# A two-layer convolution and delta-net mixer: the output's gate is spread over the partitions through DRAM instead of by products on TensorE

## The chip, the cores and the metric

The kernel runs on one core of one Trainium2 chip, which has engines for products (TensorE, "PE"; its weight loads are "PEld"), for elementwise work (VectorE, "DVE", and ScalarE, "ACT"), for general work (GpSimd, "POOL") and for issuing transfers (SyncE, "SP"). The metric is the time of one launch on the device in microseconds, lower is better. There is one core, so it is also the slowest.

## The reference, cut to what matters

Two layers (DEPTH = 2) work on 1024 tokens `x` and 256 context tokens `ctx` of 1024 channels. Each layer modulates a normalized input, projects it, runs a convolution branch and a gated delta rule of four heads, and adds the gated output projection:

```python
def modulate(x, cond, norm_w, w_ada, b_ada):
    mod = jax.nn.silu(cond) @ w_ada + b_ada
    shift, scale, gate = (jnp.expand_dims(m, -2) for m in jnp.split(mod, 3, axis=-1))
    return rms_norm(x, norm_w) * (1 + scale) + shift, gate
...
    h, gate = modulate(x, cond, norm_w, w_ada, b_ada)
    proj = h @ w_in
...
    out = jnp.concatenate([y_conv, y_dn], axis=-1) @ w_out
    return x + gate * out, s_f, s_b
```

So `gate` is one vector of 1024 numbers for each layer and condition (`c` for `x`, `c_ctx` for `ctx`). It multiplies every token's output row, channel by channel. The context has no output in the last layer, so layer 1 needs the gate for `x` alone.

## The kernel before, in words

The 1280 tokens stand in 10 blocks of 128. For each layer, 28 groups of projection weights (128 columns each) are streamed through three buffers `wst` by transfers on SP's queue, split by ScalarE (`whi`) and VectorE (`wlo`) into a 16-bit high and low part, and multiplied by the input's high and low part in three products for each of 8 slices (L376; 128x512 or 128x256).

A layer consists of steps. For head h these are K, Q, V and Z (projections; Z also writes the output gate `sgz` to `gdr` in DRAM), A (`head_a`, convolutions and norms of Q, K, V, with what the decay needs), B (`head_b1`: a 32x32 elimination on VectorE, L701 to L713, with the transposes L712 and L713 at its end, then the block inverse by small products from L729 on), D (`head_b2`, transposes and masks), R (`head_rec`, the recurrence over 10 blocks in both directions, L845 to L881) and N (`head_norm`, L894 to L924). For the convolution branch they are C (projection of a slice), T (the taps on VectorE, L528 and L538), L (`conv_norm`, layer norm of a block of tokens) and G (the convolution's gate: `sgc` to `gdr`). W (`early_wout`) loads the first two slices of the output weights. The string PLAN[l] lists the steps in the order in which they are written, and LEAD gives some of them a lead over others: the framework then sets one fixed program for each engine, in which instructions with a lead stand earlier. An engine runs its program in order, so an instruction that waits holds up all behind it.

The modulation is computed in 24 groups of 128 columns. A group's weights are loaded by `ada_load` and used by `ada_use` (L164: products with the condition; L181: VectorE adds the bias and writes two columns of `md`, one for each condition). Groups 16 to 23 are the gate. ADA_AT[l] lists the weight groups of the projection after which a modulation group is taken.

At the end of a layer comes the output: for each block of 128 tokens, `y` is loaded from `ydr` on SP (L1003), ScalarE and VectorE split it into `yh` and `yl` (L1010, L1011), the output weights are split into `woh` and `wol` (L414, L415), TensorE takes three products for each of 8 slices and two halves of 512 columns (L1022, into `pj` or `rc`), and `out_end` multiplies them by the gate (L1034, `tmp = pj * gbc`) and adds `x` (L1035). The last head's part of `y` never goes to DRAM: `head_norm` leaves it in `olast`, with eight products (L918) to spread the norm. The first two blocks are done together, and their products for the first three slices come first.

`gbc[v]` is a tile of 128x1024 with the gate of condition v on every partition (L1066 to L1075). Since `md` has the channels on the partitions, the tile is made on TensorE: for each half of 512 columns, four products take one column of `md`, repeated 128 times, as the weights and the identity as the moving side (L1071), and ScalarE copies the PSUM bank into the tile (L1074):

```python
pe.matmul(pg[:, k * 128:(k + 1) * 128],
          lhsT=md[l][:, 16 + hf * 4 + k, v:v + 1].to_broadcast([128, 128]), rhs=ident,
          start=True, stop=True)
```

Layer 0 does it for both conditions, layer 1 for one: 24 products and 6 copies. The trace keeps two records for a product of this type (4-byte operands, 128 columns).

Of the kernel before, what the change touches and what calls it, by code (L numbers as in the profile page):

```python
# [8 lines left out]
F32 = mybir.dt.float32  # L9
# [4 lines left out]
AF = mybir.ActivationFunctionType  # L14
# [4 lines left out]
DEPTH = 2  # L19
# [23 lines left out]
for _name, _w in (("nw", DEPTH * KT), ("bada", DEPTH * 24), ("cw", DEPTH * 4 * CW), ("cb", DEPTH * 4),  # L43
# [7 lines left out]


PLAN = (
# [4 lines left out]
)  # L58

ADA_AT = ((0, 2, 4, 6, 7, 8, 9, 10, 11, 12, 13, 14, 15, 16, 17, 18, 19, 20, 21, 22, 23, 24, 26, 27), (0, 3, 10, 14, 15, 16, 19, 22))


LEAD = {'O': 300, 'A': 700, 'B': 450, 'D': 1000, 'L': 1200, 'M': 0, 'N': 500, 'R': 1000, 'W': 2550}


def pos(b):
# [4 lines left out]
def mixer_kernel(ctx: ExitStack, tc: tile.TileContext, xs, cst_d, wada, win, wab, gp_d, wout, fnw, out):  # L73
    nc = tc.nc
    dve, act, pool, pe = nc.vector, nc.scalar, nc.gpsimd, nc.tensor
# [6 lines left out]
    def bank(tag, bufs, shape=(128, 512)):  # L82
        return ps.tile(list(shape), F32, tag=tag, name=tag, bufs=bufs)

    def misc(shape=(128, 512)):
        return bank("pb", 2, shape)
# [14 lines left out]
    ident = cp.tile([128, 128], F32, name="ident")  # L101
# [21 lines left out]
    xres = tc.dram_tile([T, DM], F32, name="xres")  # L123
    ydr = [tc.dram_tile([KT - 1, 128, T], F32, name=f"ydr{l}") for l in range(DEPTH)]
    cdr = [tc.dram_tile([4, 128, T], F32, name=f"cdr{l}") for l in range(DEPTH)]
    gdr = [tc.dram_tile([KT, 128, T], F32, name=f"gdr{l}") for l in range(DEPTH)]
    rdr = [tc.dram_tile([20, T], F32, name=f"rdr{l}") for l in range(DEPTH)]

# [28 lines left out]
    def bada(l, g0, g1):  # L157
        b0 = _COLS["bada"] + 24 * l
        return cst[:, b0 + g0:b0 + g1].unsqueeze(2).to_broadcast([128, g1 - g0, 2])

    def ada_mm(o, w):

        for k in range(KT):
            pe.matmul(o, lhsT=w[:, k, :], rhs=scond[:, k:k + 1, :].to_broadcast([128, 64, 2]), start=(k == 0),  # L164
                      stop=(k == KT - 1))
# [5 lines left out]
    md = [gp.tile([128, 24, 2], F32, tag=f"md{l}", name=f"md{l}") for l in range(DEPTH)]  # L171

    def ada_load(l, g):
        w = wp.tile([128, KT, 128], F32, tag="wst", name="wst", bufs=3)
        nc.sync.dma_start(w, wada[l, g])
        return l, g, w

    def ada_use(l, g, w):
        pa = bank("pw", 1, (128, 64, 2))
        ada_mm(pa, w)  # L180
        dve.tensor_tensor(out=md[l][:, g:g + 1, :], in0=pa[:, 0:1, :], in1=bada(l, g, g + 1), op=ADD)  # L181

    def ada_mod(l):
        n0 = _COLS["nw"] + KT * l
        m = md[l]
        nwb = cst[:, n0:n0 + KT].unsqueeze(2).to_broadcast([128, KT, 2])
        dve.scalar_tensor_tensor(out=m[:, 8:16, :], in0=m[:, 8:16, :], scalar=1.0, in1=nwb, op0=ADD, op1=MUL)
        dve.tensor_scalar(out=m[:, 8:16, :], in0=m[:, 8:16, :], scalar1=32.0, scalar2=None, op0=MUL)
        ss = gp.tile([128, 2], F32, tag="mss", name="mss")
        jk = gp.tile([128, 16], F32, tag="mjk", name="mjk")  # L190
        for v in range(2):
            act.activation(jk, m[:, 0:16, v], AF.Square, accum_out=ss[:, v:v + 1])
        pq = bank("pw", 1, (128, 2))
        pe.matmul(pq, lhsT=ones, rhs=ss, start=True, stop=True)
        s, inv = pow2(pq, 2, "mh")
        inv4 = gp.tile([128, 4], F32, tag="inv4", name="inv4", bufs=2)
        for i_ in range(2):
            dve.tensor_scalar(out=inv4[:, 2 * i_:2 * i_ + 2], in0=inv, scalar1=(1.0, 0.5)[i_], scalar2=None, op0=MUL)
        ab = gp.tile([128, 16, 2], F32, tag="ab", name="ab", bufs=2)
        dve.tensor_tensor(out=ab, in0=m[:, 0:16, :], in1=s.unsqueeze(1).to_broadcast([128, 16, 2]), op=MUL)  # L200
        return ab, inv4
# [129 lines left out]
    def later(n, f, *a):  # L331
        for _ in range(n):
            yield 1
        f(*a)
# [9 lines left out]
    def load_w(l, g, invh):  # L344
        prefetch((l, g))
        split((l, g))
        nxt_ = GORDER.index((l, g)) + 1

        if held:
            active.append(later(0, ada_use, *held.pop()))  # L350
        if nxt_ < len(GORDER) and GORDER[nxt_][0] == l:
            prefetch(GORDER[nxt_])
            active.append(later(0, split, GORDER[nxt_]))
        if (nxt_ - 1) % (len(GORDER) // DEPTH) in ADA_AT[l]:
            held.append(ada_load(*ADA[l].pop(0)))
        hi, lo, inv, _ = ready.pop((l, g))
        return hi, lo, unscale(inv, invh)
# [40 lines left out]
    for l in range(DEPTH):  # L398
# [65 lines left out]
        g = gp.tile([128, NB, 8], F32, tag="gg", name="gg")  # L464
# [464 lines left out]
        def emit(step):  # L929
            k, i = step[0], int(step[1:] or 0)  # L930
            if k in "KQV":
                head_proj(i, "KQV".index(k))
            elif k == "A":
                with after("elim"):
                    prep[i] = head_a(i)
            elif k == "B":
                inv[i] = head_b1(i, prep[i][0], prep[i][2])
            elif k == "D":
                b2[i] = head_b2(i, *prep[i])
            elif k == "R":  # L940
                head_rec(i, prep[i][0], prep[i][2], inv[i], *b2[i])
            elif k == "N":
                head_norm(i, prep[i][0], b2[i][2][:, 1], b2[i][3], zs[i])
            elif k == "Z":
                zs[i] = head_z(i)
            elif k == "C":
                us[i] = conv_proj(i)
            elif k == "T":
                with after("elim"):
                    conv_taps(i // 3, i % 3)  # L950
            elif k == "G":
                conv_gate(i)
            elif k == "W":
                early_wout()
            elif k == "L":
                conv_norm(i)

        for step in PLAN[l].split():
            with tc.high_priority(LEAD[step[0]]) if step[0] in LEAD else nullcontext():
                emit(step)  # L960
        while active:
            tick()
        while held:
            ada_use(*held.pop())
# [6 lines left out]
        with tc.tile_pool(name=f"op{l}", bufs=1, side="right", reuse_waits="tile") as op:  # L971
            spare = {}

            def place(tag, n=DM, dt=F32):
                if tag in spare:
                    return spare.pop(tag)[:, 0:n]
                t_ = op.tile([128, n], dt, tag=tag, name=tag, bufs=1)
                return t_[:, 0:n]
# [13 lines left out]
            def out_tile(tt, tag):  # L992
                i = (tt - xb0) % 2
                y = place(f"y{i}", 896).rearrange("p (k t) -> p k t", t=128)
                yh, yl = (place(f"{t_}{i}", DM, F32R).rearrange("p (k t) -> p k t", t=128) for t_ in ("yh", "yl"))
                return tt, y, yh, yl, [bank(tag, 2) for _ in range(2)]
# [57 lines left out]
            gbc = {}  # L1054

            with tc.high_priority(LEAD["O"]):
                two = [out_tile(xb0, "pj"), out_tile(xb0 + 1, "rc")]
# [6 lines left out]
                for k in KORDER[NEARLY + 3:]:  # L1064
                    load_wout(place, k)
            for v in ((0,) if last else (1, 0)):  # L1066
                t_ = place(f"gb{v}")
                for hf in range(2):
                    pg = misc()
                    for k in range(4):  # L1070
                        pe.matmul(pg[:, k * 128:(k + 1) * 128],  # L1071
                                  lhsT=md[l][:, 16 + hf * 4 + k, v:v + 1].to_broadcast([128, 128]), rhs=ident,
                                  start=True, stop=True)
                    act.activation(t_[:, hf * 512:(hf + 1) * 512], pg, AF.Copy)  # L1074
                gbc[v] = t_  # L1075
            if last:
                fw = place("fw")
                nc.sync.dma_start(fw, fnw.partition_broadcast(128))
# [87 lines left out]
```

## Time and profile before

| | |
|---|---|
| median of three runs | 1574.67 us (1572.23 to 1576.7) |
| profiled execution, its own time | 1572.46 us |
| its span | 1570.8 us |
| TensorE busy | 1457.3 us, 93% |
| VectorE busy | 1253.7 us, 80% |
| ScalarE busy | 896.0 us, 57% |
| POOL busy | 145.1 us, 9% |
| granted clock of TensorE, mean | 0.976 |

A share of busy time is a mean over stages with different limits. A timeline row has the start, the length, the engine, the line and operation, the tiles with their shape and a count of equal rows in succession, and in brackets how long the engine stood idle ahead of it and for whom. A clock of 1.00 means 2.4 GHz and 0.50 means 1.2 GHz.

### The profile page before, as it was taken

Reading aid. Unit: us, or ns where it says so; the run is one execution under the profiler, and the core shown is the slowest. Engines: PE = TensorE matmul, PEld = TensorE weight load, DVE = VectorE, ACT = ScalarE, POOL = GpSimd, SP = SyncE. Lnnn points to the kernel's source line nnn. Section 1 sums busy time; section 2 is a strip of 40 time slices with the busy share of each in tenths; the row PEclk is TensorE's granted clock in tenths of the full one; section 3 lists DMA queues with packets and bytes.
Section 4 is the critical chain, followed back from the end, with each engine's and each line's share of the span. In section 5 each row is a group of like instructions: output and inputs, shape, how many; then the busy total and the mean of one; then the engine's idle time right before and its main releaser. Section 6 shows DMA issues by size and latency. Waiting matters only on the chain. (4 is left out here: it accounts for less than half of the span.)

```text
span 1570.8 us, 27515 instructions
## 1 busy us (share of the span) xinstructions
PE 1457.3 (93%) x10536; PEld 991.6 (63%) x10536; DVE 1253.7 (80%) x2759; ACT 896.0 (57%) x2013; POOL 145.1 (9%) x252
## 2 busy tenths in 40 slices
PE   7899899899998999899899999999899799999997
PEld 1656577577655776676787754476467476467686
DVE  3865989899679999856676556999999989987675
ACT  3757467565347764645454337576676577576321
POOL 0002010100011101101000002010110100121000
PEclk9799999999999999999999999999999999999999
DMA  9213111311143213333743113121311312253651
GB/s 299 113 55 109 45 62 54 138 45 55 58 135 108 76 54 106 112 135 124 250 156 104 55 41 110 39 75 44 112 62 41 121 54 69 82 175 120 213 171 54
DMA packets 83328, 158.21 MB, mean 101 GB/s; under 512 B 5670, under 2 KB 52764, under 8 KB 83196
## 3 DMA queue, kind: packets, MB, share of 16 engines
q1 hardware_dynamic: 67408, 96.74, 19.8%
q0 software_dynamic: 15280, 59.52, 10.3%
q8 instruction: 83, 1.36, 0.3%
q14 instruction: 49, 0.40, 0.1%
q10 hardware_dynamic: 508, 0.19, 0.0%
HBM read 125.43 MB, written 30.99 MB: 100 GB/s over the span
## 5 line engine op out<-in xcount | busy, mean ns | idle before, releaser
L376 PE MATMUL pj<-hhi,whi 128*128 128x512 f16 (+1 forms) x1184 | 424.8, 359 | 4.2 <-ACT raw L596 3.9
L376 PE MATMUL pj<-hhi,wlo 128*128 128x512 f16 (+1 forms) x1184 | 424.4, 359 | 1.2 <-DVE wlo L300 1.1
L376 PE MATMUL pj<-hlo,whi 128*128 128x512 f16 (+1 forms) x1184 | 425.2, 359 | 0.0
L376 PEld LDWEIGHTS <-whi 128*128 128x128 f16 x2368 | 231.5, 99 | 179.3 <-issue 20.2
L538 DVE SCALAR_TENSOR_TENSOR acc<-u,cws,acc 128x960 f32<-128x960 f32 (+26 forms) x240 | 231.0, 963 | 1.2
L376 PEld LDWEIGHTS <-wlo 128*128 128x128 f16 x1184 | 117.4, 99 | 90.5 <-issue 7.9
L1022 PE MATMUL pj<-woh,yh 128*128 128x512 f32 x256 | 102.2, 399 | 7.4 <-ACT yh L1010 7.4
L1022 PE MATMUL pj<-woh,yl 128*128 128x512 f32 x256 | 103.0, 402 | 0.7 <-DVE yl L1011 0.7
L286 ACT ACTIVATE whi<-wst 128x1024 bf16<-128x1024 f32 x56 | 59.0, 1053 | 77.3 <-PE pj L376 69.5
L1022 PE MATMUL pj<-wol,yh 128*128 128x512 f32 x256 | 102.2, 399 | 0.0
L623 DVE SCALAR_TENSOR_TENSOR kq<-raw,cst,kq 128x1284 f32<-128x1284 f32 (+1 forms) x64 | 93.5, 1477 | 7.9 <-ACT kq L621 7.7
L706 DVE TENSOR_TENSOR et<-xp 128x30 f32<-128x30 f32 (+14 forms) x240 | 82.4, 343 | 5.3
L708 DVE TENSOR_TENSOR xp<-xp,et 128x30 f32<-128x30 f32 (+14 forms) x240 | 80.5, 335 | 5.3
L859 ACT ACTIVATE vs<-rc,hs 128x128 f32<-128x128 f32 x144 | 52.1, 367 | 56.1 <-PE rc L856 55.6
L300 DVE SCALAR_TENSOR_TENSOR wlo<-wst,w_s,whi 128x1024 f16<-128x1024 f32 x56 | 73.9, 1320 | 9.4 <-ACT whi L299 9.2
L299 ACT ACTIVATE whi<-wst,w_s 128x1024 f16<-128x1024 f32 x56 | 64.2, 1146 | 26.9 <-DVE w_s L298 26.3
L164 PE MATMUL pw<-scond,wst 128*128 128x128 f32 x512 | 71.7, 277 | 0.1
L164 PEld LDWEIGHTS pw<-scond,wst 128*128 128x128 f32 x512 | 64.3, 192 | 2.3 <-DVE cst__7698 L562 0.3
L866 PE MATMUL rc<-vs,ktm 128*128 128x128 f32 x288 | 60.9, 300 | 3.8 <-ACT vn L862 2.8
L866 PEld LDWEIGHTS rc<-vs,ktm 128*128 128x128 f32 x288 | 43.4, 189 | 29.8 <-ACT vn L862 23.8
L1022 PEld LDWEIGHTS pj<-woh,yh 128*128 128x128 f32 x256 | 48.9, 191 | 19.0 <-ACT yh L1010 7.8
L623 DVE SCALAR_TENSOR_TENSOR v<-raw,cst,v 128x1284 f32<-128x1284 f32 x32 | 50.0, 1561 | 13.5 <-ACT v L621 13.3
(367 smaller groups left out, 2958.7 us busy)
## 6 DMA issues: line engine op xcount, KB each, us to landing
wst<-in_win_dram SPq DMA_DIRECT2D x56, 512.0 KB
row<-rdr POOLq DMA_DIRECT2D x35, 640.0 KB, 4.5
wst<-in_wada_dram SPq DMA_DIRECT2D x32, 512.0 KB
x<-in_xs_dram SPq DMA_DIRECT2D x20, 512.0 KB
ast<-in_wada_dram SPq DMA_DIRECT2D x8, 1024.0 KB
wst<-in_wout_dram SPq DMA_DIRECT2D x16, 512.0 KB
y<-ydr SPq DMA_DIRECT2D x14, 448.0 KB
a<-cdr SPq DMA_DIRECT2D x9, 512.0 KB
```

The source lines that it names most:

```text
L164: pe.matmul(o, lhsT=w[:, k, :], rhs=scond[:, k:k + 1, :].to_broadcast([128, 64, 2]), start=(k == 0), stop=(k == KT - 1))
L286: act.activation(hi.bitcast(BF16), st, AF.Square, accum_out=ss)
L299: act.activation(hi, st, AF.Identity, scale=s[:, 0:1])
L300: dve.scalar_tensor_tensor(out=lo, in0=st, scalar=s[:, 0:1], in1=hi, op0=MUL, op1=SUB)
L376: pe.matmul(pj[:, 0:n], lhsT=a[:, k, :], rhs=b[:, k, t0:t0 + n], start=(i == 0), stop=(i == 3 * KT - 1))
L538: gates["big"] = dve.scalar_tensor_tensor(out=ao, in0=ui, scalar=cws[:, 0, j:j + 1], in1=ao, op0=MUL, op1=ADD)
L623: gates["big"] = dve.scalar_tensor_tensor(out=dst, in0=src[:, o0 + j:o0 + j + n], scalar=col("sw", j0 + j), in1=dst, op0=MUL, op1=ADD)
L706: dve.tensor_tensor(out=ev, in0=xp[:, j + 1:, j:j + 1].to_broadcast([128, ni, j]), in1=xp[:, j:j + 1, 0:j].to_broadcast([128, ni, j]), op=MUL)
L708: dve.tensor_tensor(out=xp[:, j + 1:, 0:j], in0=xp[:, j + 1:, 0:j], in1=ev, op=ADD)
L859: act.activation(vss[d], pns[d], AF.Identity, scale=hs[:, 2 + d, bs[d]:bs[d] + 1])
L866: pe.matmul(pkv, lhsT=ktm[:, bs[d], :], rhs=vss[d], start=True, stop=True)
L1022: pe.matmul(pj[hf], lhsT=a[:, k, :], rhs=w[k][:, hf * 512:(hf + 1) * 512], start=k == KORDER[0] and i == 0, stop=k == KORDER[-1] and i == 2)
```

## The change

A tile `mdr` of 2 x 8 x 128 numbers in DRAM is added for each layer. When `ada_use` has written the last group of the gate (g = 23), POOL issues a transfer for each condition that writes the eight gate columns of `md` to `mdr`. Where the products stood, POOL issues for each condition one transfer that reads the row of 1024 numbers and writes it to all 128 partitions of the gate's tile (512 KB). The 24 products and the 6 copies are gone. The same edit also moves steps in both PLAN strings, one entry of ADA_AT and four entries of LEAD (the entry M belongs to no step).

```diff
 PLAN = (
-    "Q0 K0 V0 C0 A0 K1 Q1 V1 B0 Z0 A1 D0 T0 T1 Q2 B1 R0 N0 C1 T2 D1 K2 C2 T3 V2 T4 T5 A2 R1 Z1 V3 B2 Q3 K3 C3 T6 Z3 "
-     "D2 N1 A3 T7 T8 B3 Z2 G0 T9 G2 T10 G1 R2 N2 D3 R3 T11 L0 L1 W L2 L3 N3 L4 G3",
...
+    "Q0 K0 V0 C0 A0 K1 Q1 V1 B0 Z0 D0 T0 T1 A1 Q2 R0 N0 B1 C1 T2 D1 K2 C2 T3 V2 A2 T4 R1 Z1 T5 V3 B2 Q3 K3 C3 T6 Z3 "
+     "D2 N1 A3 T7 T8 B3 Z2 G0 T9 G2 T10 G1 R2 N2 D3 R3 T11 L0 L1 L2 W L3 N3 L4 G3",
...
-     "A3 T7 Z3 Z2 T8 D2 B3 T9 T10 G2 G1 G0 R2 T11 D3 L0 L1 L2 L3 L4 R3 W N2 G3 N3",
+     "A3 T7 D2 Z3 Z2 T8 B3 T9 T10 G2 G1 G0 R2 T11 D3 L0 L1 R3 L2 L3 L4 W N2 N3 G3",
...
-LEAD = {'O': 300, 'A': 700, 'B': 450, 'D': 1000, 'L': 1200, 'M': 0, 'N': 500, 'R': 1000, 'W': 2550}
+LEAD = {'O': 400, 'A': 750, 'B': 450, 'D': 1000, 'L': 1600, 'M': 100, 'N': 500, 'R': 1000, 'W': 2350}
...
+    mdr = [tc.dram_tile([2, 8, 128], F32, name=f"mdr{l}") for l in range(DEPTH)]
...
         dve.tensor_tensor(out=md[l][:, g:g + 1, :], in0=pa[:, 0:1, :], in1=bada(l, g, g + 1), op=ADD)
+        if g == 23:
+
+            for v in ((0, 1) if l < DEPTH - 1 else (0,)):
+                nc.gpsimd.dma_start(mdr[l][v].rearrange("g c -> c g"), md[l][:, 16:24, v])
...
             for v in ((0,) if last else (1, 0)):
-                t_ = place(f"gb{v}")
-                for hf in range(2):
-                    pg = misc()
-                    for k in range(4):
-                        pe.matmul(pg[:, k * 128:(k + 1) * 128],
-                                  lhsT=md[l][:, 16 + hf * 4 + k, v:v + 1].to_broadcast([128, 128]), rhs=ident,
-                                  start=True, stop=True)
-                    act.activation(t_[:, hf * 512:(hf + 1) * 512], pg, AF.Copy)
-                gbc[v] = t_
+                gbc[v] = place(f"gb{v}")
+                nc.gpsimd.dma_start(gbc[v], mdr[l][v:v + 1].rearrange("v g c -> v (g c)").partition_broadcast(128))
```

In layer 1's string the first part also moves A0 behind C0, D0 ahead of A1, and A2 and C2 ahead of T3. The order of the weight groups is the same. In the programs, layer 0 differs from about 280 us of the old trace to 345 and at the gate, layer 1 from about 1205 us to its end; the rest is equal row for row. Lines of the after kernel are numbered one higher from L126 on, six higher behind `ada_use` (five higher than before, to L1071), so L381 is the old L376 and L1027 the old L1022.

TensorE's program at the start of layer 0's output, before (`md_105` is layer 0's modulation, `woh_`, `wol_`, `yh_`, `yl_` the split weights and input):

```order
L164 MATMUL pw<-scond,wst 128x128 x8
L1071 MATMUL pb<-ident,md_105 128x128 x6
L194 MATMUL pw<-mss,ones 128x2
L1071 MATMUL pb<-ident,md_105 128x128 x2
L292 LDWEIGHTS onesb
L292 MATMUL pw<-wss,onesb 128x1
L1022 MATMUL pj<-woh_7530,yh_7882 128x512
L1022 MATMUL pj<-wol_7531,yh_7882 128x512
L1071 MATMUL pb<-ident,md_105 128x128 x8
L1022 MATMUL pj<-woh_7530,yl_7883 128x512
L1022 MATMUL pj<-woh_7530,yh_7882 128x512
```

and after:

```order
L165 MATMUL pw<-scond,wst 128x128 x8
L199 MATMUL pw<-mss,ones 128x2
L297 LDWEIGHTS onesb
L297 MATMUL pw<-wss,onesb 128x1
L1027 MATMUL pj<-woh_7578,yh_7886 128x512
L1027 MATMUL pj<-wol_7579,yh_7886 128x512
L1027 MATMUL pj<-woh_7578,yh_7886 128x512
L1027 MATMUL pj<-woh_7578,yl_7887 128x512
L1027 MATMUL pj<-wol_7579,yh_7886 128x512
```

The 16 gate products are gone, and output products follow where the last eight stood.

TensorE's program at the end of layer 1 before, where the last products of the convolution's gate (L376) meet the output:

```order
L376 MATMUL pj<-hhi,whi 128x512
L376 LDWEIGHTS whi
L376 MATMUL pj<-hlo,whi 128x512
L376 LDWEIGHTS wlo
L376 MATMUL pj<-hhi,wlo 128x512
L1071 MATMUL pb<-ident,md_106 128x128 x8
L1022 MATMUL pj<-woh_15136,yh_15293 128x512
L1022 MATMUL pj<-wol_15137,yh_15293 128x512
L1022 MATMUL pj<-woh_15136,yh_15293 128x512
L1022 MATMUL pj<-woh_15136,yl_15294 128x512
```

and after (L923 is the old L918, the products of `olast`):

```order
L381 LDWEIGHTS whi
L381 MATMUL pj<-hlo,whi 128x512
L381 LDWEIGHTS wlo
L381 MATMUL pj<-hhi,wlo 128x512
L923 MATMUL pb<-ident,ost 128x128 x8
L1027 MATMUL pj<-woh_15119,yh_15276 128x512
L1027 MATMUL pj<-wol_15120,yh_15276 128x512
L1027 MATMUL pj<-woh_15119,yh_15276 128x512
L1027 MATMUL pj<-woh_15119,yl_15277 128x512
```

The gate's products are gone, and the projection's products now all stand ahead of L923.

VectorE's program at the end of the last head's elimination before (L706 and L708 are its steps, L712 and L713 its transposes):

```order
L181 TENSOR_TENSOR md_106<-pw,cst 128x2
L706 TENSOR_TENSOR et<-xp 128x30
L708 TENSOR_TENSOR xp<-xp,et 128x30
L296 TENSOR_SCALAR w_i<-pw 128x1
L712 STREAM_TRANSPOSE xnat<-xp 128x32x32
L713 STREAM_TRANSPOSE xtr<-xp 128x32x32
L298 TENSOR_SCALAR w_s<-w_i 128x1
L538 SCALAR_TENSOR_TENSOR acc<-u,cws,acc 128x64
```

and after, a few steps earlier in the same elimination (L711 and L713 are its steps now):

```order
L595 TENSOR_SCALAR gcs<-wm 128x1
L713 TENSOR_TENSOR xp<-xp,et 128x10x21
L711 TENSOR_TENSOR et<-xp 128x198
L305 SCALAR_TENSOR_TENSOR wlo<-wst,w_s,whi 128x1024
L713 TENSOR_TENSOR xp<-xp,et 128x9x22
L608 SCALAR_TENSOR_TENSOR sgz<-sgz,pj 128x512
L711 TENSOR_TENSOR et<-xp 128x184
```

The split `wlo` of a weight group (L305) and a step of `sgz` (L608) now stand inside the elimination, where before they followed it.

## Rows read from the trace of the kernel before

**Rows 1.** The page's busy time by engine, and its costliest groups (busy, mean ns).

```profile
PE 1457.3 (93%) x10536; PEld 991.6 (63%) x10536; DVE 1253.7 (80%) x2759; ACT 896.0 (57%) x2013; POOL 145.1 (9%) x252
...
L300 DVE SCALAR_TENSOR_TENSOR wlo<-wst,w_s,whi 128x1024 f16<-128x1024 f32 x56 | 73.9, 1320 | 9.4 <-ACT whi L299 9.2
```

**Rows 2.** TensorE's waits: line, what it waited for, us, times, longest.

```profile
PE pb L729 <- DVE xtr L713: 17.0, 6, 4.2
...
PE pj L1022 <- ACT yh L1010: 7.4, 2, 5.2
...
PE rc L880 <- DVE na L832: 2.5, 1, 2.5
```

**Rows 3.** Timeline of TensorE, 728 to 765 us: start, length, [idle before].

```profile
748.92 1.50 PE L1071 MATMUL pb<-ident,md 128*128 128x128 f32 x12
...
750.70 0.69 PE L1071 MATMUL pb<-ident,md 128*128 128x128 f32 x4
...
756.55 0.79 PE L1022 MATMUL pj<-woh,yh 128*128 128x512 f32 x1 [5.16 <-ACT yh L1010]
...
757.57 3.73 PE L1071 MATMUL pb<-ident,md 128*128 128x128 f32 x16
760.96 0.67 PE L1022 MATMUL pj<-woh,yl 128*128 128x512 f32 x1
```

**Rows 4.** Windows: busy of PE, PEld, DVE, ACT, POOL; PEclk, DMA share, GB/s.

```profile
755.00:760.00 5.00, 3.45 (x13) 2.98 (x14) 3.96 (x9) 2.94 (x8) 0.00 (x0) 0.50 1.10 323
...
770.00:775.00 5.00, 5.00 (x23) 4.03 (x22) 0.01 (x1) 1.15 (x2) 0.00 (x0) 1.00 1.11 335
...
1470.00:1475.00 5.00, 4.26 (x12) 3.28 (x12) 5.00 (x15) 3.70 (x8) 0.00 (x0) 0.66 0.97 341
250.00:300.00 50.00, 46.70 (x317) 33.75 (x316) 46.38 (x123) 26.18 (x70) 6.21 (x10) 1.00 0.34 119
```

**Rows 5.** Timelines of ScalarE, POOL, SyncE and VectorE at the output of layer 0.

```profile
755.98 1.01 ACT L1010 ACTIVATE yh<-y 128x384 fp32r<-128x384 f32 x2 [0.78 <-DMA y<-ydr]
...
749.52 0.55 POOL L591 DMA_DIRECT2D gdr<-sgc  x1 [4.39 <-DVE md L187]
...
749.62 1.57 SPq L1003 DMA_DIRECT2D y<-ydr  x3
...
775.59 0.69 DVE L1034 TENSOR_TENSOR tmp<-pj,gb 128x512 f32<-128x512 f32 x1 [5.58 <-PE pj L1022]
```

**Rows 6.** Timelines of TensorE, VectorE and ScalarE at the end of layer 1.

```profile
1464.79 0.38 PE L376 MATMUL pj<-hhi,wlo 128*128 128x512 f16 x1
1465.01 1.95 PE L1071 MATMUL pb<-ident,md 128*128 128x128 f32 x16
...
1470.90 0.50 PE L1022 MATMUL pj<-woh,yl 128*128 128x512 f32 x1 [0.74 <-DVE yl L1011]
...
1462.62 0.69 DVE L924 TENSOR_TENSOR olast<-kq,pb 128x512 f32<-128x512 f32 x1 [0.20 <-PE pb L918]
...
1466.88 3.50 DVE L415 TENSOR_TENSOR wol<-wst,woh 128x1024 fp32r<-128x1024 f32 x3 [0.26 <-ACT woh L414]
...
1465.21 0.69 ACT L586 ACTIVATE sgc<-pj,wm 128x512 f32<-128x512 f32 x1 [8.76 <-PE pj L376]
```

**Rows 7.** Timeline of TensorE, layer 1, heads 2 and 3: rows that waited.

```profile
1226.88 0.27 PE L903 MATMUL pa<-ident,ost 128*8 128x128 f32 x1 [2.61 <-DVE ost L145]
...
1242.28 1.04 PE L729 MATMUL pb<-xtr,tt 32*32 32x32 f32 x40 [2.35 <-DVE xtr L713]
...
1354.87 0.18 PE L292 MATMUL pw<-wss,onesb 128*128 128x1 bf16 x1 [0.70 <-DVE md L181]
...
1359.08 0.82 PE L729 MATMUL pb<-xtr,tt 32*32 32x32 f32 x40 [1.42 <-DVE w_s L298]
```

**Rows 8.** Timeline of TensorE: two steps of the last head's recurrence begin.

```profile
1404.74 0.49 PE L851 MATMUL rc<-S,kq 128*128 128x128 f32 x2
...
1409.03 0.39 PE L851 MATMUL rc<-S,kq 128*128 128x128 f32 x2
```

More of the change, by code (lines that the diff above doesn't have):

```diff
@@ L53 @@
 PLAN = (
[4 rows of a table removed]
-)
-ADA_AT = ((0, 2, 4, 6, 7, 8, 9, 10, 11, 12, 13, 14, 15, 16, 17, 18, 19, 20, 21, 22, 23, 24, 26, 27), (0, 3, 10, 14, 15, 16, 19, 22))
-LEAD = {'O': 300, 'A': 700, 'B': 450, 'D': 1000, 'L': 1200, 'M': 0, 'N': 500, 'R': 1000, 'W': 2550}
[4 rows of a table added]
+)
+ADA_AT = ((0, 2, 4, 6, 7, 8, 9, 10, 11, 12, 13, 14, 15, 16, 17, 18, 19, 20, 21, 22, 23, 24, 26, 27), (0, 3, 10, 14, 15, 16, 17, 22))
+LEAD = {'O': 400, 'A': 750, 'B': 450, 'D': 1000, 'L': 1600, 'M': 100, 'N': 500, 'R': 1000, 'W': 2350}
 def pos(b):
```

2 rows, old and new, of the table PLAN are left out of this document.

## Prediction

> **What bounds the kernel now.** I read the page's table of engines first: TensorE is busy 93% of the span [rows 1], so the time is TensorE's work plus its waits. Work that TensorE no longer does is worth its length only where TensorE was not waiting anyway, and work moved from one place to another is worth only the waits that it fills. So the second view is TensorE's list of waits [rows 2]: the 40 small products of the block inverse (L729) wait 17.0 us for the last transpose of the elimination on VectorE (L713), and the output's products (L1022) wait 7.4 us for `yh`. The change touches both places. The third view is TensorE's timeline at both ends of a layer, with the windows around it [rows 3 to 6], where the gate's products stand; the fourth is the timeline of the two stretches in which the order code moved (before the inverses of layer 1's last heads, and the last head's recurrence) [rows 7, 8].
>
> The profiled execution took 1572.46 us (its span and 1.7 us around it). The median of the three runs is 1574.67, 2.2 us above. The sum below is a difference against the profiled execution; I set it on the median, since that is the figure to which the changed kernel's is compared.
>
> **The gate in layer 0 (A).** Before, 16 gate records (eight products of two records each, the first half of the gate) stand ahead of the output: 12 of them run at 748.92 in 1.50 us, 4 more at 750.70 [rows 3]. After them TensorE idles 5.16 us until `yh` is there, at 756.55. To take these 16 away makes the idle longer and moves no end: 0. The other 16 stand between the second and the third product of the output, start at 757.57 and let the third start at 760.96: 3.4 us, because the granted clock is 0.50 from 755 to 760 [rows 4] (the lower of the two levels, 1.2 GHz, after that idle). In the after program output products stand there. At full clock the 16 take 1.95 us, as at 1465.01 [rows 6]. If the clock comes back at the same moment, the removed 3.4 us at the lower clock let the output start that much work earlier, but at the lower clock: worth 1.95 us at the full one. So -1.95, and -3.4 if the clock comes back with the work rather than at a moment of its own.
>
> Against it stand the two broadcasts of 512 KB each, on POOL's queue right behind the last `gdr<-sgc`, which went at 749.52 [rows 5]. Three `y` loads are issued from 749.62, and `yh` had to wait 0.78 us for the last of them [rows 5]: the landing of `y` ends the 5.16 us wait. The DMA engines are full there, share 1.10 at 323 GB/s from 755 to 760 [rows 4]. No row of before has two queues contending for this landing. If the broadcasts hold `y` back by nothing: +0. If all of them goes ahead: 1.05 MB / 335 GB/s (the rate at 770 to 775) = +3.1 us. Most of the `y` bytes are asked for at the same time as the broadcasts, so I take a third: +1.0. A is -1.95 + 1.0 = -1.0, ends -3.4 and +1.2. The Trainium skill ("DMA: Bandwidth & Descriptors", section "Queues, rings and completion order") says that each DMA engine takes turns between the queues it has work for, a packet at a time; by that rule about half of the broadcasts' bytes pass ahead of the loads' end, an estimate of +1.6, and A would be -0.4 and the sum -3.1. No run here shows it yet. The result of the broadcasts isn't needed until 775.59 [rows 5], 25 us later, so the broadcasts as such are hidden; so is the POOL write of `mdr`, whose data leave an adaLN step a head or more before the gate, in the order of either layer. `mdr` is written in 4-byte pieces, of which no row shows the like: between the 0.55 us of any issue [rows 5] and eight times that for its eight columns, on an engine that is no bound: 0 to +1, I take 0.
>
> **The gate and the tail in layer 1 (B, F).** Here the gate's 16 records run at 1465.01 for 1.95 us, inside TensorE's wait for the first output products [rows 6]. Removing them saves nothing by itself. But the order also changes: 22 products stood behind the sums before, 10 ahead of the L918 products and 12 behind; after it is 6 ahead and none behind. In the trace `sgc` on ScalarE waits 8.76 us for the last of the 12, to 1465.21, and the VectorE copies `wol` follow at 1466.88; the third kind of output product, with `yl`, starts at 1470.90 [rows 6]. With no product behind L918, `wol` can follow `olast`, that ends at 1463.3 [rows 6]: the tail is 1466.88 - 1463.3 = 3.5 us shorter. The 16 products are 16 x 0.22 = 3.5 us of TensorE (1464.79 to 1465.01 is one) [rows 6], and they run earlier. Net 0. Idle at the end is longer, so the lower clock can last as much again as it cost (0.34 of the 5 us from 1470 to 1475, 1.7 us [rows 4]): ends 0 and +1.7.
>
> **Layer 0, head 0 to head 1 (C).** Nine more products stand ahead of N0's transposes, one fewer ahead of the inverse. VectorE is busy 46.4 of 50 us from 250 to 300 [rows 4] and sets when the inverse goes on; the same VectorE rows stand ahead of L713 as before. So 0, ends -1.9 (nine products at 0.22, if TensorE had waited that long there) and +1.7 (the clock's cost of B, if a wait opens elsewhere).
>
> **Layer 1, head 2 (D).** Ahead of the inverse stand four more projection products and two small ones, 1.3 us, while TensorE waits there 2.35 us for L713 [rows 7]. VectorE has the same rows ahead. So the wait falls by 1.3: -1.3. Ahead of N1's transposes (wait 2.61 us [rows 7]) stand 8 more products and four small ones, 2.6 us; those are products that before filled the time before L713, so they count once. Ends 0 and -2.6.
>
> **Layer 1, head 3 (E).** Before the inverse 36 more projection products stand, 8.0 us at 0.22 each and a small one. The waits there are 0.70 and 1.42 us [rows 7]. VectorE has 2.5 us more to do ahead of L713 (one `wlo` of 1.32 us [rows 1], one `sgz` of 512 columns at the 0.69 us of such a row [rows 5] and three of a few columns), which the 8.0 us cover. -2.1. The products are taken from later places: in the recurrence, by counting the order's rows and their lengths, five steps keep only 4.0 to 4.7 us of TensorE work, where before two had 3.8. The shortest step in the trace took 1409.03 - 1404.74 = 4.29 us [rows 8], so the short ones lack 0.3 + 0.1 + 0.3 = 0.7 us. E is -1.4; ends -2.6 and +3 (five steps at half a microsecond more).
>
> **The sum.** -1.0 + 0 + 0 - 1.3 - 1.4 = -3.7. On the median: 1574.67 - 3.7 = 1571.0, or 0.23% less, which is within 0.3%, about what a measurement of this kernel can tell from no change (0.3% is 4.7 us: faster is below 1569.9, slower above 1579.4).
>
> **Rivals.**
> Clearly faster: the new order does its job in full. The waits of rows 7 all vanish (2.61 + 2.35 + 0.70 + 1.42 = 7.1) and layer 0's second half of the gate gives its 3.4 us with no delay of `y`: -10.5, 1564.2. For it: TensorE gets more work ahead at each of these places, and 48 gate records are truly gone. Against it: the products are taken from other places, where VectorE and ScalarE are nearly as busy. Chance 0.35; with the lower end of my own case, faster has 0.42.
> Slower: the last head's recurrence loses its cover. In it TensorE, VectorE and ScalarE hand one state on, and the five short steps have ScalarE's and VectorE's work of the layer norm (L0 to L4) standing between their own, in the order written. If each of the five waits as long as the longest single wait of a recurrence in the trace, 2.5 us at L880 [rows 2], that is +12.5 in place of the 0.7: -3.7 + 11.8 = +8.1, 1582.8. It decides from 4.7 + 4.4 = 9.1 us over the five steps, 1.8 us each. For it: those five steps stand close together. Against it: TensorE was busy nearly throughout these stretches. Chance 0.13. The Trainium skill ("TensorE: Matmul & The Clock Gate", section "What's actually happening") states that the throttled clock is the default and that activity releases it; by that, gate products were activity in an idle stretch, and idle steps would cost again at the lower clock: the trace agrees in that the 5.16 us idle is followed by 0.50.
> No effect: the broadcasts cost what the products gave (A at +1.2), and the moved products are taken from places where they filled as much (D and E at 0): +1.2, 1575.9. Chance 0.12, within 0.3%.
>
> **How the numbers follow.** My own case (1568 to 1574, its A, D and E between half and whole) has 0.40. Faster by over 0.3%: 0.42 (the faster rival, and the lower end of mine). Within 0.3%: 0.45. Slower by over 0.3%: 0.13. The range reaches from the faster rival with C's end added (1564.2 - 1.9 = 1562.3, as 1562) to the no-effect case with the ends of B and C added (1575.9 + 1.7 + 1.7 = 1579.3); what lies outside is most of the slower rival and little else.
>
> **What would show it.** A: the third output product of layer 0 starts near 758.5 on the old clock of times, `yh` no more than 1.0 us later than before, and granted clock 0.50 in that stretch. F: the first `wol` of layer 1 about as late behind `olast` as 0.2 us. D and E: the waits of L729 for L713 in heads 2 and 3 of layer 1 near 1.0 and 0. The forecast is wrong if `yh` in layer 0 comes 2 us later, if the last recurrence shows waits over 2 us a step, or if TensorE's waits in layer 1's second half fall by more than 5 us.

## The result

The changed kernel takes 1591.03 us in the median of four runs (1585.56 to 1592.71), the kernel before 1575.68 (1572.23 to 1577.20) beside it: ratio 1.0087, 95% interval [1.0064, 1.0109], so by the ratio 13.7 us slower [10, 17] (the two medians are 15.4 us apart). The forecast was 1571.0 with 1562 to 1579.3: wrong, on the side of the slower rival, and not by that rival's mechanism. In the profiled execution the span grew from 1570.8 to 1588.0 us.

The page of the changed kernel, its span and engines, answering [rows 1]:

```profile
span 1588.0 us, 27445 instructions
...
PE 1462.6 (92%) x10488; PEld 990.1 (62%) x10488; DVE 1251.1 (79%) x2759; ACT 893.9 (56%) x2007; POOL 149.3 (9%) x258
```

The 48 gate records are gone, and TensorE is still busy 5.3 us longer in all, since more of its work ran at the lower clock (granted clock 0.967 in the mean, 0.976 before); the rest of the 17.2 us is idle time. The list of TensorE's waits, answering [rows 2]:

```profile
PE pb L734 <- DVE xtr L718: 25.5, 7, 9.6
...
PE pj L1027 <- ACT yh L1015: 5.0, 2, 4.3
...
PE pj L1027 <- DVE yl L1016: 3.0, 1, 3.0
...
PE rc L885 <- DVE na L837: 2.2, 1, 2.2
```

L734 is the old L729, L718 the old L713. The wait for the end of the elimination grew by 8.5 us, and its longest one is now 9.6. To see where the time was lost, the starts of the same steps are set side by side (from TensorE's timelines; us; the end of an inverse is its first closing product, L771, now L776):

| step | before | after | later by |
|---|---|---|---|
| layer 0, inverse of head 0 | 185.11 | 184.38 | -0.7 |
| layer 0, inverse of head 1 | 308.82 | 313.61 | 4.8 |
| layer 0, first output product | 756.55 | 763.79 | 7.2 |
| layer 1, inverse of head 2 | 1242.28 | 1250.29 | 8.0 |
| layer 1, end of head 3's inverse | 1376.09 | 1401.28 | 25.2 |
| layer 1, first output product | 1469.20 | 1483.36 | 14.2 |
| layer 1, last output product | 1561.06 | 1578.27 | 17.2 |

Three places stand out: head 1's inverse in layer 0, head 3's in layer 1 (of which some 11 us come back, since products stand ahead of it that stood behind it before), and the output of layer 1. The 2.4 us between head 1's inverse and layer 0's output are less than the 3.2 us (446.3 and 449.5) by which that stretch differs between two of the kernels below that have the same program there, so I don't read them.

**Layer 0, head 1.** First VectorE's wait from 225 to 350 us and TensorE's row behind it, then POOL's timeline there (after; L714 is a memset of the diagonal, L675 a masked selection on POOL):

```profile
DVE xnat L717 <- POOL xp L714: 7.4, 1, 7.4
```

```profile
313.61 1.28 PE L734 MATMUL pb<-xtr,tt 32*32 32x32 f32 x40 [9.61 <-DVE xtr L718]
```

```profile
294.00 1.83 POOL L186 DMA_DIRECT2D mdr<-md  x2 [3.15 <-DVE md L182]
295.82 1.11 POOL L927 DMA_DIRECT2D ydr<-kq  x2
296.92 0.54 POOL L670 DMA_DIRECT2D row<-rdr  x1
297.45 0.54 POOL L927 DMA_DIRECT2D ydr<-kq  x1
308.34 1.32 POOL L675 TENSOR_SCALAR_AFFINE_SELECT na<-row 128x1280 f32<-128x1280 f32 x1 [10.35 <-DMA row<-rdr]
309.60 0.16 POOL L714 MEMSET xp<- 128x32 f32 x1
```

The same stretch of POOL before (L665, L670, L709 are those lines):

```profile
294.31 0.54 POOL L665 DMA_DIRECT2D row<-rdr  x1
294.85 0.54 POOL L922 DMA_DIRECT2D ydr<-kq  x1
302.52 1.31 POOL L670 TENSOR_SCALAR_AFFINE_SELECT na<-row 128x1280 f32<-128x1280 f32 x1 [7.14 <-DMA row<-rdr]
304.06 0.16 POOL L709 MEMSET xp<- 128x32 f32 x1 [0.22 <-DVE xp L708]
```

The row that the selection needs is issued at 296.92 and the selection can start 11.4 us later, against 8.2 us before. The memset stands behind the selection in POOL's program, VectorE's two closing transposes behind the memset, and TensorE's inverse behind those. So the chain from TensorE's wait leads over VectorE and POOL back to a load that stands behind two `mdr` writes of 4 KB. VectorE was done with the elimination at 302.4, earlier than before, and waited.

### The profile page after: what moved, and what is told of

The parts are those of the page before. It is cut to its first block, busy times and chain, and to the rows that moved or that the text cites. A ratio compares the mean times of both kernels' runs of the same rounds, so it can differ in the third digit from the quotient of the medians.

```text
span 1588.0 us, 27445 instructions
## 1 busy us (share of the span) xinstructions
PE 1462.6 (92%) x10488; PEld 990.1 (62%) x10488; DVE 1251.1 (79%) x2759; ACT 893.9 (56%) x2007; POOL 149.3 (9%) x258
## 5 line engine op out<-in xcount | busy, mean ns | idle before, releaser
L381 PE MATMUL pj<-hhi,whi 128*128 128x512 f16 (+1 forms) x1184 | 426.7, 360 | 6.0 <-ACT raw L601 5.1
L381 PE MATMUL pj<-hlo,whi 128*128 128x512 f16 (+1 forms) x1184 | 426.7, 360 | 0.0
L381 PE MATMUL pj<-hhi,wlo 128*128 128x512 f16 (+1 forms) x1184 | 426.1, 360 | 0.0
L381 PEld LDWEIGHTS <-whi 128*128 128x128 f16 x2368 | 232.8, 100 | 179.7 <-issue 22.5
L381 PEld LDWEIGHTS <-wlo 128*128 128x128 f16 x1184 | 117.9, 100 | 90.1 <-issue 9.2
L1027 PE MATMUL pj<-woh,yh 128*128 128x512 f32 x256 | 103.8, 405 | 5.0 <-ACT yh L1015 5.0
L1027 PE MATMUL pj<-woh,yl 128*128 128x512 f32 x256 | 104.2, 407 | 3.0 <-DVE yl L1016 3.0
L1027 PE MATMUL pj<-wol,yh 128*128 128x512 f32 x256 | 103.6, 405 | 0.0
L713 DVE TENSOR_TENSOR xp<-xp,et 128x30 f32<-128x30 f32 (+14 forms) x240 | 82.5, 344 | 5.4
L711 DVE TENSOR_TENSOR et<-xp 128x30 f32<-128x30 f32 (+14 forms) x240 | 80.1, 334 | 5.2
L305 DVE SCALAR_TENSOR_TENSOR wlo<-wst,w_s,whi 128x1024 f16<-128x1024 f32 x56 | 72.7, 1298 | 12.4 <-ACT whi L304 12.1
L601 ACT ACTIVATE raw<-pj,wm 128x512 f32<-128x512 f32 (+1 forms) x68 | 42.0, 617 | 33.5 <-PE pj L381 32.3
L628 DVE SCALAR_TENSOR_TENSOR v<-raw,cst,v 128x1284 f32<-128x1284 f32 x32 | 49.9, 1560 | 13.5 <-ACT v L626 13.3
```

What stands on the lines that cost most here:

```text
L305: dve.scalar_tensor_tensor(out=lo, in0=st, scalar=s[:, 0:1], in1=hi, op0=MUL, op1=SUB)
L381: pe.matmul(pj[:, 0:n], lhsT=a[:, k, :], rhs=b[:, k, t0:t0 + n], start=(i == 0), stop=(i == 3 * KT - 1))
L628: gates["big"] = dve.scalar_tensor_tensor(out=dst, in0=src[:, o0 + j:o0 + j + n], scalar=col("sw", j0 + j), in1=dst, op0=MUL, op1=ADD)
L711: dve.tensor_tensor(out=ev, in0=xp[:, j + 1:, j:j + 1].to_broadcast([128, ni, j]), in1=xp[:, j:j + 1, 0:j].to_broadcast([128, ni, j]), op=MUL)
L713: dve.tensor_tensor(out=xp[:, j + 1:, 0:j], in0=xp[:, j + 1:, 0:j], in1=ev, op=ADD)
L1027: pe.matmul(pj[hf], lhsT=a[:, k, :], rhs=w[k][:, hf * 512:(hf + 1) * 512], start=k == KORDER[0] and i == 0, stop=k == KORDER[-1] and i == 2)
```

## The experiments

Theory P/W: the write of `mdr`, in pieces of 4 bytes, delays transfers that are waited for. Rival G: the gate through DRAM costs by itself, through the missing TensorE work and the broadcasts. Rival O: the new order costs, whatever the gate does. The first four runs separate the parts. "Before" beside a run is its median in the same comparison.

**The gate alone, in the old order** (PLAN, ADA_AT and LEAD of before).

> The gate through DRAM, with the step order, leads and adaLN places of the kernel before. In this program the two mdr writes of layer 0 stand on POOL behind the row load that head 1's masked selection needs, not ahead of it. Theory P (the mdr write on POOL's queue delays that load, the selection, the memset behind it and so the end of head 1's elimination): no 7 us wait of VectorE for POOL there; total within 3 us of before, 1573 to 1579. Rival G (the DRAM gate costs by itself at both layer ends, through a longer idle and the lower clock): 6 to 10 us over before wherever the write stands, 1582 to 1586. Rival O (the new order alone is what costs): as before within 3 us.

Measured: 1579.79 us (before 1577.01), ratio 1.0021 [1.0000, 1.0041]. In that program the row load goes at 293.32, ahead of the writes, and the selection starts at 300.03: no wait for POOL. So here the write did no harm in layer 0. G's 6 to 10 us were not there (the interval is 0 to 6.5 us).

**The new order alone, gate by products.**

> The new step order, leads and adaLN places, with the gate by products on TensorE as before; no mdr. Theory P: layer 0's 4.8 us before head 1's inverse is not there (wait of TensorE for L713 about 4 us instead of 9.6), layer 1's loss of some 8 us from head 2 on stays: about 1582. Rival O: all of the loss stays, 1588 to 1592. Rival G: the loss is gone, 1572 to 1577.

Measured: 1580.03 us (before 1577.01), ratio 1.0022 [1.0010, 1.0034]. Head 1's inverse started 0.2 us later than before, counted from the start of head 0's, with a wait of 3.4 us. The two parts cost 0.2% each when alone and 0.9% together: O falls; the sum of the parts, 0.4%, falls short as well, though there the ends of the intervals meet.

**The write on SyncE's queue.**

```diff
-                nc.gpsimd.dma_start(mdr[l][v].rearrange("g c -> c g"), md[l][:, 16:24, v])
+                nc.sync.dma_start(mdr[l][v].rearrange("g c -> c g"), md[l][:, 16:24, v])
```

> The changed kernel, with the mdr write issued on SyncE's queue instead of POOL's. Theory P: VectorE no longer waits 7.4 us for POOL's memset in head 1 of layer 0 (0 to 2.5 us left), 4 to 6 us below the changed kernel: 1585 to 1587. Rivals G and O: as the changed kernel, 1588 to 1593.

Measured: 1593.51 us (before 1577.01), ratio 1.0106 [1.0085, 1.0126]. A miss, and the useful one: with no write on POOL's queue, the row load (issued at 298.25) let the selection start only at 312.23, after 14.0 us. So the delay doesn't need POOL's queue; it is in something that the queues share, and what the DMA engines did meanwhile is shown further down.

**The write done twice.**

```diff
+                nc.gpsimd.dma_start(mdx[l][v].rearrange("g c -> c g"), md[l][:, 16:24, v])
```

> The changed kernel with each mdr write done twice on POOL, the second time into a tile that nobody reads. Theory P: the row load behind the writes is issued about 1 to 2 us later and lands later by 2 to 4 us, VectorE's wait for POOL in head 1 grows from 7.4 to 9 to 11 us: 1593 to 1596. Rivals G and O: as the changed kernel, 1588 to 1593.

Measured: 1613.14 us (before 1577.01), ratio 1.0235 [1.0213, 1.0257], so about 23 us over the changed kernel, far more than expected; VectorE's wait for POOL in head 1 was 13.5 us and the landing of a write 18.7 instead of 11.2. The direction is theory P's, its size was not.

The next four take the write apart from the gate.

**The writes added to a kernel whose gate is still by products** (nobody reads `mdr`), in the new order and in the old one:

> The new order with the gate by products on TensorE, plus the mdr writes as in the changed kernel, which nobody reads. Theory W (the write of 1024 pieces of 4 bytes fills the DMA engines for some 10 us, and what lands meanwhile lands late): head 1's inverse in layer 0 starts 5 us later than in the same kernel without the writes, and the total is most of the way to the changed kernel: 1587 to 1592. Rival G (what costs is the missing TensorE work and the broadcasts at the layers' ends): as the new order alone, 1578 to 1582.

> The kernel before plus the mdr writes, which nobody reads; in its order they stand on POOL behind the row load of head 1. Theory W: no transfer that is waited for in layer 0 is in flight behind them, so head 1's inverse is on time; in layer 1 they meet the sgz writes, 2 to 5 us: 1577 to 1582. Rival G: as before, 1573 to 1578.

Measured: 1591.55 us, 1.0093 [1.0071, 1.0114], in the new order; 1586.50, 1.0060 [1.0036, 1.0084], in the old (before 1576.08 for both). With the new order the unread writes alone make the whole loss. In the old order they cost more than expected (and more than the 1.0021 of the gate alone, which holds the same writes; the intervals touch, so the size there, 3 to 9 us, stays open).

The expectation that head 1 would be on time in the old order failed, too. The row load, issued at 294.82, 1.1 us ahead of the writes, landed after 11.0 us, and VectorE waited 2.9 us for POOL; in the gate alone, where POOL's program is the same, it landed after 6.6 us. In the trace's records of single DMA packets, those of the writes began 1.2 us before the load's last one was over (300.64 and 301.84), in the gate alone 0.5 us before (299.14 and 299.63). It is one profile each, but a place behind the load in the program did not protect it here.

**The write in eight pieces of 512 bytes**, in the new order and in the old one. The columns are transposed by one small product first:

```diff
-                nc.gpsimd.dma_start(mdr[l][v].rearrange("g c -> c g"), md[l][:, 16:24, v])
+                pt = bank("pw", 1, (8, 128))
+                pe.transpose(pt, md[l][:, 16:24, v], ident)
+                mt = hd.tile([4 * NB, 128], F32, tag="rt", name="mt", bufs=1)[0:8]
+                act.activation(mt, pt, AF.Copy)
+                nc.gpsimd.dma_start(mdr[l][v], mt)
```

> The changed kernel, but the gate's columns are transposed on TensorE first (one small product and one ScalarE copy a condition), so mdr is written in eight pieces of 512 bytes. Theory W: the landing of 4-byte pieces is gone, VectorE's wait for POOL in head 1 falls from 7.4 to under 2.5 us, no long wait in layer 1's last inverse beyond the new order's own: 1577 to 1582. Rival G: 1588 to 1593.

> The old order with the gate through DRAM, written in pieces of 512 bytes after a transpose on TensorE. Theory W: without the small pieces the gate through DRAM costs nothing or gains 1 to 4 us: 1571 to 1577. Rival G: 3 us over before, as the old order with the 4-byte write: 1578 to 1582.

Measured: 1578.88 us, 1.0014 [1.0001, 1.0028], and 1577.66, 0.9997 [0.9981, 1.0014] (before 1576.08). Theory W holds: with wide pieces the loss falls from 0.87% to 0.14% in the new order (in the old one from 0.21% to nothing, which is within the intervals). G falls: the gate through DRAM neither costs nor gains anything clear of the noise. The write now also stands behind the row load in POOL's program, so this pair alone doesn't separate width from place; the next does.

**Fewer pieces, and wider pieces, at the same place** (new order, gate by products, unread writes):

```diff
-                nc.gpsimd.dma_start(mdr[l][v].rearrange("g c -> c g"), md[l][:, 16:24, v])
+                nc.gpsimd.dma_start(mdr[l][v][0:4].rearrange("g c -> c g"), md[l][:, 20:24, v])
```

```diff
-                nc.gpsimd.dma_start(mdr[l][v].rearrange("g c -> c g"), md[l][:, 16:24, v])
+                nc.gpsimd.dma_start(mdr[l][v], md[l][:, 16:24, :].rearrange("c g v -> c (g v)"))
```

> The new order with the gate by products on TensorE and unread writes at the places of the changed kernel, but of half as many pieces: 512 pieces of 4 bytes a condition instead of 1024. If the pieces' number sets the cost (theory W): the landing falls from 11 to some 6 us, the total is about half way between the new order alone (1580) and the same with whole writes (1591.5): 1583 to 1588. If it is a fixed cost of a write at that place in POOL's queue: 1589 to 1593.

> As the last, with two unread writes at the same places in layer 0 and one in layer 1, but of 128 pieces of 64 bytes each (twice the bytes, an eighth of the pieces). If the pieces' number sets the cost: the landing is 2 to 3 us, VectorE's wait for POOL in head 1 under 2.5 us, the total near the new order alone: 1578 to 1583. If the write as such costs, by its place in the queue: 1589 to 1593.

Measured: 1591.05 us, 1.0080 [1.0052, 1.0108], for 512 pieces of 4 bytes; 1578.72, 1.0010 [0.9991, 1.0029], for 128 pieces of 64 bytes (before 1576.31). At the same place in POOL's program, twice the bytes in wider pieces cost nothing, so it is not the place of the write by itself. But half the pieces cost about as much as all, which theory W in its simple form (the count sets the cost) did not expect. The 64-byte write has wider pieces, fewer of them (128), and each from one partition, where a row of 4-byte pieces mixes 128 partitions; the runs don't separate these any further. The issues of the two kernels, from the page's list of DMA issues (KB each, us to landing), first the half write, then the 64-byte one:

```profile
mdr<-md POOLq DMA_DIRECT2D x3, 2.0 KB, 13.1
```

```profile
mdr<-md POOLq DMA_DIRECT2D x3, 8.0 KB, 4.5
```

The whole 4-byte write took 13.0 us at the same place, and the 512-byte one, which stands elsewhere in POOL's program, 3.0. In layer 0 two writes go back to back; the single one of layer 1 took 10.8 us with the whole and 11.3 with the half write. What the engines did meanwhile, in windows of 5 us (the last three columns are granted clock, DMA share and GB/s): the new order alone, then with the whole unread write.

```profile
300.00:305.00 5.00, 5.00 (x25) 2.25 (x23) 4.62 (x15) 0.00 (x0) 0.28 (x1) 1.00 0.65 202
```

```profile
295.00:300.00 5.00, 5.00 (x30) 2.74 (x28) 4.86 (x12) 0.51 (x1) 3.51 (x6) 1.00 1.38 212
300.00:305.00 5.00, 4.57 (x22) 1.86 (x19) 2.57 (x11) 0.00 (x0) 0.00 (x0) 1.00 0.75 33
```

With the write the DMA engines are busy 0.75 of the stretch and move 33 GB/s, where they moved 202 at a share of 0.65. The records of single packets show what stood still. The writes' own 32 packets of 256 bytes took 0.08 to 0.50 us each and were over by 298.72. The 160 packets of 4096 bytes of the three `ydr<-kq` behind them, which write to DRAM as well, took up to 7.25 us each and 139 us in sum (0.21 and 26 us in the new order alone), and the row load between them landed 13.6 us after its issue (6.2). So the engines were held by what came behind the small pieces; why that stood still, no run shows.

**Layer 1's gate by products, layer 0's through DRAM** (512-byte pieces), in either order. This tests a second loss, at the output of layer 1, and looks for a version that beats both kernels.

> The new order, layer 0's gate through DRAM written in pieces of 512 bytes, layer 1's gate by products on TensorE as before. If removing the products at layer 1's end costs there (a wait of 2.97 us for yl and the lower clock after it, against 0.85 us and the full clock in the new order with the products): from the first L918 products to the last output product 94 us instead of 96.7, the total some 2 us below the same kernel with both layers through DRAM: 1574 to 1578. If those 2.6 us are only how one profile fell: the same within 1 us, 1577 to 1581.

> The old order, with layer 0's gate through DRAM in pieces of 512 bytes and layer 1's by products. In the old order the products stood inside a wait at that end and the tail was 0.3 us shorter than without them: 1574 to 1578, the same as before, and not clearly below the old order with both through DRAM.

Measured: 1576.15 us, 1.0009 [0.9989, 1.0029], and 1576.43, 0.9994 [0.9978, 1.0009] (before 1576.71). Neither beats the kernel before, and the first, at 1.0009, is not clear of the same kernel with both layers through DRAM, at 1.0014. So the second loss shows in the profiles alone: TensorE's timeline at the end of layer 1, first after the change, then the new order with layer 1's products (L1084 the gate, L1031 the output):

```profile
1480.62 2.02 PE L923 MATMUL pb<-ident,ost 128*128 128x128 f32 x16 [1.28 <-DVE ost L146]
1483.36 0.50 PE L1027 MATMUL pj<-woh,yh 128*128 128x512 f32 x1 [0.72 <-ACT yh L1015]
...
1487.29 0.80 PE L1027 MATMUL pj<-woh,yl 128*128 128x512 f32 x1 [2.97 <-DVE yl L1016]
1487.88 0.63 PE L1027 MATMUL pj<-wol,yh 128*128 128x512 f32 x1
```

```profile
1469.49 2.02 PE L927 MATMUL pb<-ident,ost 128*128 128x128 f32 x16 [1.28 <-DVE ost L146]
1471.40 2.05 PE L1084 MATMUL pb<-ident,md 128*128 128x128 f32 x16
1473.20 0.48 PE L1031 MATMUL pj<-woh,yh 128*128 128x512 f32 x1
...
1474.92 0.40 PE L1031 MATMUL rc<-wol,yh 128*128 128x512 f32 x1
1476.16 0.73 PE L1031 MATMUL pj<-woh,yl 128*128 128x512 f32 x2 [0.85 <-DVE yl L1020]
1476.73 0.40 PE L1031 MATMUL pj<-woh,yh 128*128 128x512 f32 x1
```

Without the gate's products TensorE runs three output products, waits 2.97 us for `yl`, and its next products take 0.63 us each, at the lower clock (granted clock 0.50 from 1487.3 to 1491.5). With them the program that the framework writes is another: eight products stand ahead of the first `yl`, the wait is 0.85 us, and the products behind it take 0.40 us (granted clock 1.00 from 1476.1 to 1480.0). In both the first product with `yl` starts 6.7 us behind the first L918 product, so what was removed only became a wait. From the first L918 product to the last output product the new order took 94.1 us in all five kernels with the products and 96.6 to 97.9 in all four without: 2.5 to 3.8 us for removing work. In the old order there is no such difference: 99.8 to 101.7 us in three kernels with them, 100.9 and 101.7 in two without. The Trainium skill ("TensorE: Matmul & The Clock Gate", section "What's actually happening") says that the throttled clock is the default and that activity releases it; the two stretches above, 0.50 behind the long wait and 1.00 behind the short one, agree.

## Why the prediction was wrong, step by step

**The write of `mdr` (in A): taken at 0, ends 0 and +1. This step failed.** In the changed order its cost was 11.5 us (the new order with the unread writes, 1591.55, less the new order alone, 1580.03) or 0.0071 of the time by the ratios, 11 us. I had costed the writing engine's issue time, and argued that the data are not needed for a long time. Both hold: the issues took 0.9 us each, and nobody waited for `mdr`. What I left out is who else uses the DMA engines while it lands: 11.2 us in the median for 4 KB, while the row load landed after 11.4 us instead of the 6.2 of the new order alone. The order showed the two writes ahead of the row load on POOL, and in the trace of before that load ended a wait of POOL of 7.14 us; I followed POOL no further, since it is busy 9% [rows 1], and none of the three signs that I named for a wrong forecast looks there. I had drawn on the Trainium skill for the queues' turns but not for its line on small pieces ("DMA: Bandwidth & Descriptors", section "Specifications": below 512 bytes a write costs a read as well). The runs agree that small pieces are dear at 4 bytes, and not at 64: a size far below that limit cost nothing that could be measured.

In layer 1 the same write works by another path. ScalarE's waits around head 3's inverse, after:

```profile
ACT sgz L607 <- DMA gdr<-sgz: 5.0, 1, 5.0
```

`sgz` has one buffer; its transfer to `gdr` was issued at 1367.32, behind the write at 1363.05, and ScalarE could go on at 1376.31, 9.0 us later, where such a transfer lands in 2.3 us in the median; by the records of single packets its data moved only from 1374.35 on. Behind that instruction in ScalarE's program stand the copies that the block inverse needs. The wait is 7.0 us with the unread writes, 1.0 in the new order alone and 0.5 before.

**The gate's products and the broadcasts (A): -1.0. About right.** The gate through DRAM without small pieces, in the old order, is 0.9997 of before [0.9981, 1.0014], so between -3 and +2 us. Its inner terms weren't as I had them. `yh` was not held back: ScalarE took it right behind `woh`, without a wait for `y` (first row; [rows 5] had 0.78 us), so the +1.0 for the broadcasts was 0. And the output's first products stayed at the lower clock to 768.9, so the removed 3.4 us [rows 3] were partly taken up by slow output products:

```profile
763.23 0.92 ACT L1015 ACTIVATE yh<-y 128x384 fp32r<-128x384 f32 x2
```

```profile
763.79 0.80 PE L1027 MATMUL pj<-woh,yh 128*128 128x512 f32 x1 [4.30 <-ACT yh L1015]
764.39 0.63 PE L1027 MATMUL pj<-wol,yh 128*128 128x512 f32 x1
```

From the first to the twelfth output product TensorE took 5.2 us, where it had taken 6.8: 1.6 us saved, near the 1.95 of the sum.

The Trainium skill's rule on the queues' turns, by which A would have been -0.4, made no difference that could be seen here.

**Layer 1's end (B, F): 0 with ends 0 and +1.7. The sum held, its parts did not.** That `wol` follows `olast` at once was right (1483.28, with the last `olast` from 1482.67), and from the first L918 product to the first one with `yl` it took 6.7 us, where it had been 10.3 with 12 products between. From the first L918 product to the last output product the kernel before took 100.5 us, so the four kernels in the new order without the products are 2.6 to 3.9 us shorter, where I had 3.5 less up to 1.7. But "removing them saves nothing by itself" was too kind: against the same order with the products it costs 2.5 to 3.8 us. I had taken the order of the output products behind them as given; it changes with them.

**Layer 0, head 1 (C): 0. Right for the order** (0.2 us in the new order alone), and then undone by the write.

**Layer 1, heads 2 and 3 (D, E): -1.3 and -1.4. Wrong in sign.** The new order alone costs 0.22%, 3.5 us [1.6, 5.4], and 0.10 and 0.14% with the 64-byte and the 512-byte writes beside it. In its profile TensorE waited 3.4 us for L713 at head 2, where I had seen 1.0, and 2.4 us at head 3, where I had seen the wait covered; the inverse of head 3 started 7.6 us later relative to head 2's ([rows 7] has both before):

```profile
1248.45 0.82 PE L729 MATMUL pb<-xtr,tt 32*32 32x32 f32 x40 [3.42 <-DVE xtr L713]
...
1372.84 0.82 PE L729 MATMUL pb<-xtr,tt 32*32 32x32 f32 x40 [2.38 <-DVE xtr L713]
```

VectorE's longest wait there, new order alone, and its windows from one inverse to the other (the third busy figure is VectorE's), first before, then the new order alone:

```profile
DVE na L832 <- PE pb L829: 6.5, 1, 6.5
```

```profile
1242.00:1359.00 117.00, 109.48 (x886) 72.16 (x886) 108.86 (x224) 79.67 (x185) 10.01 (x16) 0.99 0.19 62
```

```profile
1248.00:1372.00 124.00, 116.70 (x915) 74.89 (x915) 110.45 (x227) 81.13 (x187) 10.89 (x17) 0.99 0.20 67
```

VectorE has 1.6 us more work there, and stands idle 5.4 us more (8.14 us, now 13.55), which the one wait of 6.5 us for head 2's score products (L829) covers; before it had no wait of that kind. TensorE began those products no later behind head 2's inverse than before, 33.5 against 33.9 us. What changed is VectorE's program: it has 27.5 us of work between that inverse and the scores, where it had 31.6, so it came to them early, stood, and had more left to do behind them, ahead of head 3's elimination. This is read from one profile of each kernel; no run tests it. I had counted the rows ahead of L713 and not asked what they wait for in turn. The five thin steps of the recurrence, the slower rival's mechanism, showed no wait of TensorE over 2.2 us in the changed kernel and are not the cause.

## What to carry to other kernels

A transfer is not free because nobody waits for its data. Look at what else is in flight while it lands and who waits for that, above all for a scatter of single numbers: transpose first and write wide pieces. A place just behind the awaited load was not enough here (2.9 us of VectorE's time). When an edit takes instructions out, the program that a scheduler writes behind them changes too; compare the rows behind the gap, not only the gap. And when work is moved ahead of an engine's wait, follow it one engine further: the program of the engine that ends the wait has changed too, and it may now stand at a place where it did not wait before.

## What the runs showed of the hardware

A write of 4 KB in 1024 pieces of 4 bytes landed in 11.2 to 13.0 us (the median of three, in four kernels), one of 2 KB in 512 such pieces in 13.1 us, one of 8 KB in 128 pieces of 64 bytes in 4.5 us, and one of 4 KB in 8 pieces of 512 bytes in 3.0 to 4.4 us in four kernels. In 5 us while the 4-byte writes were on their way, the engines were 0.75 busy at 33 GB/s; single packets of 4096 bytes of writes to DRAM behind them took up to 7.25 us, where the longest took 0.21 in the same order without the writes. That half the pieces took as long as all is not explained here. The delay is there as well when the write is issued on another queue: the row load landed after 13.4 us with the write on SyncE's queue, after 11.4 and 13.6 with it on POOL's, and after 6.2 without it.
